# Output stage of a hybrid decoder layer: residual gate on result columns, final gain ahead of the norm, one store per row tile

## The chip, the cores and the metric

One core of one Trainium2 chip runs the whole layer as one program. The metric is the device time of one execution in microseconds; for the kernel before, three timed runs gave 243.9, 244.47 and 245.1 us (median 244.47).

## What is computed

One decoder layer for 512 tokens of width 1024, all in float32. The end of it is what the change is about:

```python
mod = c_act @ w_mod[l] + b_mod[l]
shift, scale, gate = jnp.split(mod, 3, axis=-1)
...
y_attn = rmsnorm(attn, attn_out_gain[l]) * jax.nn.silu(z_attn)
y_lru = rmsnorm(rec, lru_out_gain[l]) * jax.nn.silu(z_lru)
y = jnp.concatenate([y_attn, y_lru], axis=-1) @ w_out[l]
x = x + gate[:, None, :] * y
return rmsnorm(x, final_gain)
```

`gate` is one number per output column (1024 of them). Before this end stand the modulated norm, one input projection, block-sparse attention (8 heads) and a gated recurrence (512 channels).

## The kernel before, in words

**Tiles and stages.** Tokens are four row tiles of 128. Every large product is made exact enough by three passes: a weight or an activation `w` is split into a rounded part `wh` and a rest `wl` (function `split`: a copy that casts, then a subtraction of 1024 columns, L246, on VectorE), and `mm3` (L237 to L240) issues three matmuls. The stages are: the modulation and the norm, the first seven column blocks of the input projection (`acc`), then 17 units (`UNITS`: 13 weight blocks `wc0` to `wc12` and four of `v`) with attention (`sc` scores, `z` softmax, `tp` transposes, `av`) and the recurrence woven in, and last the output stage from `T_OUT` on.

**What sets the order.** The program is written as a list of operations with due times. `Plan.emit` (L93) is a list scheduler in the host program: it walks a clock with estimated costs, and for each engine picks the operation that can begin first and is due first. The result is one fixed order per engine and for SP's queue of transfers; the engines follow it and wait for each other by semaphores. An operation with `alt` may go to either VectorE or ScalarE. A changed cost, due time or operation anywhere can so move operations far away from it.

**The gate.** `gate_col` (L498) loads one block of the gate's weights (`wgt`, 512 KB) and multiplies it with `cb`, summing along the row (L501): 8 instructions of 128x1024 on VectorE with 8 small additions (L503). `gate_row` (L506) turns the columns into a row that stands on every partition, `grow` [128, 1024].

**The output stage** (L697 to L771). Four groups `g`: attention half times left and right columns, recurrent half times left and right columns. Each loads two blocks of `w_out` (`wo`), **multiplies them with `grow`** (L710, 8 instructions of 128x1024 on VectorE) and splits them. Then, for each row tile, 12 matmuls fill one PSUM bank `po`, and one instruction (L727) scales it by the branch's norm (`rba`, `rbl`), adds the residual `xr` and writes `xr`. In the recurrent groups ScalarE squares `xr` with a running sum (L738) into `ssq`; the left half times the final gain `fg` goes to `oa` (L743). When a row tile's right half is there, ScalarE takes the root (L750), VectorE the reciprocal (L753), ScalarE scales `oa` (L758), VectorE makes `ob` from `xr`, the norm and `fg` (L761), and each half is stored on its own (L768, L770, 256 KB each). The last row tile is cut in two at 256 columns: its second group of matmuls has 256 columns, and it leaves in four stores of 128 KB, one of them on ScalarE's queue (L765).

Of the kernel before, what the change touches and what calls it, by code (L numbers as in the profile page):

```python
# [56 lines left out]
class Plan:  # L57
# [35 lines left out]
    def emit(self, make):  # L93
# [80 lines left out]
def tile_hymba_block(ctx: ExitStack, tc: tile.TileContext, x, wss, wgt, win0, wv, winr,  # L174
# [460 lines left out]
    for n in range(3):  # L635
        recur(n, T_REST + 44.47 + n)
    for j in range(8):
        gate_col(j, T_REST + 38.31 + 6.64 * j)
# [4 lines left out]
    t_att = [T_REST + 13.0 + 5.8 * n if n < 8 else
# [55 lines left out]
    branch_rms("a", T_OUT + 2)
    for g in range(4):  # L700
        br, half = "al"[g // 2], g % 2
        s = slice(half * 512, (half + 1) * 512)
# [4 lines left out]
        for j in range(2):
            w = t4(f"wo{g}{j}", F32, (128, 2, 512))
            load(w, wo[2 * g + j], t0 - 11 + 2 * j)
            op("V", dv(1024), lambda w=w, s=s: V.tensor_mul(  # L710
                w[:], w[:], grow[:, None, s].to_broadcast([128, 2, 512])), [w, grow], [w], t0 - 7 + 2 * j)
            wos.append(split(w, like(w), f"wo{g}{j}", 1024, t0 - 5 + 2 * j))
        for t in range(NT):
            m = slice(t * 128, (t + 1) * 128)
            cuts = (0, 256, 512) if g == 3 and t == NT - 1 else (0, 512)
            for n, (lo, up) in enumerate(zip(cuts, cuts[1:])):
                ps, w = bank("po"), up - lo
                c0, c1 = half * 512 + lo, half * 512 + up
                t1 = t0 + 2.6 * t + 2.6 * lo / 512
                for k in range(4):  # L720
                    yh, yl = Y[br, k]
                    wh, wl = wos[k // 2]
                    op("PE", 3 * pe(w), lambda k=k, ps=ps, yh=yh, yl=yl, wh=wh, wl=wl, m=m, lo=lo, up=up: mm3(
                        ps[:, :up - lo], yh[:, m], yl[:, m], wh[:, k % 2, lo:up], wl[:, k % 2, lo:up], k == 0, k == 3),
                       [yh, yl, wh, wl], [ps], t1 + 0.65 * k * w / 512)
# [4 lines left out]
                if br == "a":  # L730
                    continue
                o, q = t2("o"), half + n
                if w < 512:
                    op("V", dv(w, 1), lambda t=t, c0=c0, c1=c1, o=o, q=q: V.scalar_tensor_tensor(
                        o[:, :c1 - c0], res[t][:, c0:c1], 1.0, res[t][:, c0:c1], op0=OP.mult, op1=OP.mult,
                        accum_out=ssq[t][:, q:q + 1]), [res[t]], [ssq[t], o], t1 + 0.2)
                else:
# [2 lines left out]
                if half == 0:  # L740
                    op("V", 0.1, lambda t=t: V.tensor_scalar(
                        ssq[t][:, 0:1], ssq[t][:, 0:1], 1.0 / D, EPS, op0=OP.mult, op1=OP.add), [ssq[t]], [ssq[t]], t1 + 4)
                    op("V", dv(512), lambda t=t: V.tensor_mul(outa[t][:], res[t][:, 0:512], fg[:, 0:512]),  # L743
                       [res[t], fg], [outa[t]], t1 + 5)
                elif c1 < D:
                    op("V", 0.1, lambda t=t, q=q: V.scalar_tensor_tensor(
                        ssq[t][:, 0:1], ssq[t][:, q:q + 1], 1.0 / D, ssq[t][:, 0:1], op0=OP.mult, op1=OP.add),
                       [ssq[t]], [ssq[t]], t1 + 0.6)
                else:
                    op("A", 0.2, lambda t=t, q=q: A.activation(ssq[t][:, 3:4], ssq[t][:, q:q + 1], AF.Sqrt,  # L750
                                                               bias=ssq[t][:, 0:1], scale=1.0 / D),
                       [ssq[t]], [ssq[t]], t1 + 0.3, "sqrt")
                    op("V", 0.1, lambda t=t: V.reciprocal(ssq[t][:, 3:4], ssq[t][:, 3:4]), [ssq[t]], [ssq[t]], t1 + 0.4)  # L753
                    step = 256 if t == NT - 1 else 512
                    t1 += 1.5 if t == NT - 2 else 0.0
                    for e in range(0, 512, step):
                        sa, sb = slice(e, e + step), slice(512 + e, 512 + e + step)
                        op("A", ac(step, 1), lambda t=t, sa=sa: A.activation(  # L758
                            outa[t][:, sa], outa[t][:, sa], AF.Copy, scale=ssq[t][:, 3:4]),
                           [ssq[t], outa[t]], [outa[t]], t1 + 1.5)  # L760
                        op("V", dv(step, 1), lambda t=t, sa=sa, sb=sb: V.scalar_tensor_tensor(  # L761
                            outb[t][:, sa], res[t][:, sb], ssq[t][:, 3:4], fg[:, sb], op0=OP.mult, op1=OP.mult),
                           [res[t], ssq[t], fg], [outb[t]], t1 + 1.5)
                        if t == NT - 1 and e:
                            op("A", 0.1, lambda t=t, sa=sa: A.dma_start(out[t * 128:(t + 1) * 128, sa], outa[t][:, sa]),  # L765
                               [outa[t]], [], t1 + 2)
                        else:
                            op("SP", step / 700, lambda t=t, sa=sa: SP.dma_start(  # L768
                                out[t * 128:(t + 1) * 128, sa], outa[t][:, sa]), [outa[t]], [], t1 + 2)
                        op("SP", step / 700, lambda t=t, sa=sa, sb=sb: SP.dma_start(  # L770
                            out[t * 128:(t + 1) * 128, sb], outb[t][:, sa]), [outb[t]], [], t1 + 2)  # L771
# [75 lines left out]
```

## Time and profile before

| | |
|---|---|
| Timed runs | 243.9, 244.47, 245.1 us |
| The profiled execution | 246.51 us, of which the span from first to last instruction is 244.7 us |
| TensorE busy | 228.2 us, 93% of the span |
| VectorE busy | 208.4 us, 85% |
| ScalarE busy | 159.7 us, 65% |
| Granted clock, mean | 0.994 of full speed |

All places in time below are microseconds from the start of that span. The profiled execution's 246.51 us are 2.0 us above the median of the timed runs; 1.8 us of it lie outside the span.

### The profile page before, as it was taken

To read this page: it belongs to the slowest core of one execution; us is meant where nothing else is said; L and a number is where in the kernel's file an instruction comes from. 1 tells how busy PE (TensorE), PEld (TensorE's weight loads), DVE (VectorE), ACT (ScalarE), POOL (GpSimd) and SP (SyncE) were. 2 spreads that over 40 slices of the span, in tenths; PEclk is the share of its full clock that TensorE was granted. 3 is DMA by queue.
4 is the path that set the end of the run, shared out by engine and by line. 5 is a ranking of instruction groups with operands and counts; after the bars stand their busy time and mean duration, and the time that the engine had idled before them with its cause. 6 is when DMAs were issued, how large, how long until landed. Compare 5 with 4: busy or idle time off the path is not lost.

```text
span 244.7 us, 3163 instructions
## 1 busy us (share of the span) xinstructions
PE 228.2 (93%) x1076; PEld 181.6 (74%) x1076; DVE 208.4 (85%) x419; ACT 159.7 (65%) x273; POOL 6.6 (3%) x30
## 2 busy tenths in 40 slices
PE   1679999999999999999799999999999999999990
PEld 1557888888888778678577787867776888888880
DVE  2699999957998998898999999779899999956564
ACT  5686666842748899999951488867999530312362
POOL 0000000045000000000000000000000000000000
PEclk9999999999999999999999999999999999999997
DMA  6999999910292169931528228873650000000035
GB/s 176 342 415 411 419 409 412 410 71 3 55 265 71 39 171 385 392 127 47 171 43 214 88 43 228 331 258 108 212 197 3 0 0 0 0 3 0 1 148 195
DMA packets 13551, 41.98 MB, mean 172 GB/s; under 512 B 1632, under 2 KB 2272, under 8 KB 13024
## 3 DMA queue, kind: packets, MB, share of 16 engines
q1 hardware_dynamic: 13392, 41.66, 48.7%
q8 instruction: 8, 0.13, 0.2%
q10 hardware_dynamic: 144, 0.13, 0.2%
q14 instruction: 7, 0.06, 0.1%
HBM read 35.50 MB, written 2.10 MB: 154 GB/s over the span
## 4 chain that ended last, share of the span: by engine, by line
PE 82%; ACT 9%; DVE 4%; DMA 2%; issue 1%; SPq 1%; ACTq 0%
PE acc L394 17%; PE pj L238 11%; PE pj L240 11%; PE pj L239 10%; PE po L238 6%; PE po L240 6%; PE po L239 6%; PE tp L570 3%; PE av L560 3%; DMA x<-in_x_dram 2%; PE sc L533 2%; PE sc L530 2%; PE xp L336 2%; ACT L541 2%; ACT z L541 1%; PE gt L238 1%
## 5 line engine op out<-in xcount | busy, mean ns | idle before, releaser
L541 ACT ACTIVATE z<-z,mn 128x128 f32<-128x128 f32 (+3 forms) x32 | 17.8, 560 | 1.5 <-DVE mn L538 1.4
L538 DVE CUSTOM_DVE_ANT_0 z<-sc,cst 128x128 f32<-128x128 f32 (+3 forms) x32 | 14.8, 486 | 3.3 <-PE sc L533 3.3
L363 DVE SCALAR_TENSOR_TENSOR ws<-ws,cb 128x1024 f32<-128x1024 f32 x14 | 17.1, 1228 | 0.0
L738 ACT ACTIVATE o<-xr 128x512 f32<-128x512 f32 x7 | 4.4, 633 | 11.8 <-DVE xr L727 11.8
L228 ACT COPY pt<-tp 128x128 f32<-128x128 f32 (+3 forms) x28 | 10.3, 419 | 2.7 <-PE tp L570 2.5
L541 ACT ACT_TABLE_LOAD x9 | 11.5, 1283 | 0.1
L570 PE MATMUL tp<-ident,z 128*128 128x128 f32 x80 | 11.6, 273 | 0.0
L727 DVE SCALAR_TENSOR_TENSOR xr<-po,rbl,xr 128x512 f32<-128x512 f32 (+1 forms) x9 | 6.2, 691 | 6.3 <-PE po L240 6.2
L570 PEld LDWEIGHTS tp<-ident,z 128*128 128x128 f32 x80 | 9.6, 140 | 2.5 <-issue 0.2
L501 DVE SCALAR_TENSOR_TENSOR wgt<-wgt,cb 128x1024 f32<-128x1024 f32 x8 | 9.8, 1219 | 0.0
L710 DVE TENSOR_TENSOR wo<-wo,grow 128x1024 f32<-128x1024 f32 x8 | 9.8, 1219 | 0.0
L560 PE MATMUL av<-pt,v 128*64 128x512 f32 (+3 forms) x64 | 9.6, 439 | 0.0
L462 DVE SCALAR_TENSOR_TENSOR xc<-xl,vec,xc 128x511 f32<-128x511 f32 (+2 forms) x12 | 9.0, 747 | 0.1
L590 ACT ACT_TABLE_LOAD x7 | 9.0, 1283 | 0.1
L549 DVE TENSOR_SCALAR z<-z,rs 128x384 f32<-128x384 f32 (+3 forms) x23 | 8.4, 393 | 0.6
L336 PE MATMUL xp<-ident,x 128*128 128x128 f32 x28 | 6.7, 427 | 2.0 <-DVE x L332 2.0
L560 PEld LDWEIGHTS av<-pt,v 128*64 128x64 f32 x64 | 4.8, 136 | 5.0 <-issue 3.9
L336 PEld LDWEIGHTS xp<-ident,x 128*128 128x128 f32 x28 | 5.6, 224 | 3.2 <-DVE x L332 2.8
L550 ACT ACTIVATE z<-z,rs 128x128 f32<-128x128 f32 (+3 forms) x9 | 4.8, 530 | 4.3 <-DVE rs L544 4.2
L308 PE MATMUL cp<-ident,ccol 128*128 128x128 f32 x8 | 1.9, 424 | 5.0 <-DMA ident<-in_consts_dram 5.0
L590 ACT ACTIVATE sz<-pj 128x512 f32<-128x512 f32 x8 | 4.8, 599 | 2.1 <-PE pj L240 2.0
L541 ACT ACTIVATION_READ_ACCUMULATOR z<-z,mn 128x1 f32 x32 | 6.1, 191 | 0.0
(1087 smaller groups left out, 764.7 us busy)
## 6 DMA issues: line engine op xcount, KB each, us to landing
wc<-in_winr_dram SPq DMA_DIRECT2D x13, 512.0 KB, 5.5
ws<-in_wss_dram SPq DMA_DIRECT2D x4, 1024.0 KB, 11.0
wgt<-in_wgt_dram SPq DMA_DIRECT2D x8, 512.0 KB, 6.0
wo<-in_wo_dram SPq DMA_DIRECT2D x8, 512.0 KB, 4.4
w<-in_win_dram SPq DMA_DIRECT2D x8, 448.0 KB, 9.0
ws<-in_wss_dram SPq DMA_DIRECT2D x6, 512.0 KB, 8.4
x<-in_x_dram SPq DMA_DIRECT2D x4, 512.0 KB, 6.5
wv<-in_wv_dram SPq DMA_DIRECT2D x4, 512.0 KB, 11.7
```

What stands on the lines that cost most here:

```text
L228: op("A", acp(n) if psum else ac(n), lambda: A.copy(dst(), src()), r, w, due, after=after, alt=("V", dv(n) if psum else dv2(n), lambda: V. ...
L238: PE.matmul(ps, lh, rh, start=start, stop=False)
L239: PE.matmul(ps, lh, rl, start=False, stop=False)
L240: PE.matmul(ps, ll, rh, start=False, stop=stop)
L336: op("PE", 0.2, lambda t=t, d=d: PE.transpose(xps[d][:, t * 128:(t + 1) * 128], xt[t][:, d * 128:(d + 1) * 128], ident[:]), [xt[t], ident] ...
L363: op("V", dv(1024), lambda d=d, j=j, sc=sc: V.scalar_tensor_tensor(part(d, j), part(d, j), 1.0, cb[:], op0=OP.mult, op1=OP.mult, accum_out ...
L394: PE.matmul(acc[j][:], a[:, j * 128:(j + 1) * 128], b[:], start=first, stop=last),
L538: op("V", dv(n) + 0.085, lambda s=s, z=z: V.tensor_tensor_reduce(out=z[:, :n], in0=ps[s][:, :n], in1=cst[:, 1536 - n:1536], op0=OP.add, op ...
L541: op("A", ac(n, 1, 1), lambda s=s, z=z: A.activation(z[:, :n], z[:, :n], AF.Exp, bias=mn[s][:, 0:1], scale=-1.0, accum_out=sm[:, s:s + 1]) ...
L560: PE.matmul(ps2[64 * s:64 * s + 64, k * 128:], vt[k][:, (2 * p + s) * 64:(2 * p + s + 1) * 64], pts[s][:, k, k * 128:], start=(k == 0), st ...
L570: PE.transpose(tp[:, k * 128:(k + 1) * 128], z[:, k * 128:(k + 1) * 128], ident[:])
L590: op("A", acp(512), lambda: A.activation(z[:], ps[:], AF.Silu), [ps], [z], due, "silu")
```

## The change

Five things are done:

1. `wo` is no longer multiplied with `grow`. Instead the result is: for the attention groups (`attention_part`) ScalarE or VectorE copies `po` out with the branch norm into a tile `ua` (L717, L718), VectorE multiplies it with `grow` (L719) and adds it to `xr` (L720); for the recurrent groups (`recurrent_part`) one VectorE instruction makes `u` = po x norm x `grow` (L725) and another adds it to `xr` (L729).
2. The final gain is multiplied in before the norm for both halves: `ot` = `xr` x `fg` (L732).
3. When the norm is known, one instruction of 128x1024 scales `ot` in place: on ScalarE for row tiles 0 to 2 (L753), on VectorE for the last (L750), and one store of 512 KB per row tile sends it (L756): three on SP's queue, that of row tile 2 on ScalarE's. Row tile 2 is scaled after the last row tile's root.
4. The last row tile is cut at 320 columns and not at 256; both squares are on ScalarE.
5. Due times: the 8 `gate_col` are due from `T_OUT - 52` on in steps of 6, which is `T_REST + 75.84` in the scheduler's clock (before: from `T_REST + 38.31` in steps of 6.64), `gate_row` 2 us after `T_OUT` and not 23.5 before it; the output stage's own due times are stretched a little; the attention branch's squares may no longer go to VectorE.

```diff
-        gate_col(j, T_REST + 38.31 + 6.64 * j)
-    gate_row(0, T_OUT - 23.51)
-    gate_row(1, T_OUT - 23.51 + 2)
+        gate_col(j, T_OUT - 52 + 6 * j)
+    gate_row(0, T_OUT + 2)
+    gate_row(1, T_OUT + 3)
...
+    def attention_part(t, c, ps, t1):
+        u, r = scaled[t], rb["a"]
+        op("A", acp(512, 1), lambda: A.activation(u[:, c], ps[:], AF.Copy, scale=r[:, t:t + 1]), [ps, r], [u], t1,
+           alt=("V", dv(512, 1), lambda: V.tensor_scalar(u[:, c], ps[:], r[:, t:t + 1], None, op0=OP.mult)))
+        op("V", dv(512), lambda: V.tensor_mul(u[:, c], u[:, c], grow[:, c]), [u, grow], [u], t1 + 8)
+        op("V", dv(512), lambda: V.tensor_add(res[t][:, c], res[t][:, c], u[:, c]), [u, res[t]], [res[t]], t1 + 9)
+    def recurrent_part(t, c, q, ps, t1):
+        op("V", dv(w, 1), lambda: V.scalar_tensor_tensor(
+            u[:, :w], ps[:, :w], r[:, t:t + 1], grow[:, c], op0=OP.mult, op1=OP.mult), [ps, r, grow], [u], t1)
...
+        op("V", dv(w), lambda: V.tensor_add(res[t][:, c], res[t][:, c], u[:, :w]), [u, res[t]], [x1], t1 + 0.1)
+        op("A", ac(w, 0, 1), lambda: A.activation(o[:, :w], res[t][:, c], AF.Square, accum_out=ssq[t][:, q:q + 1]),
...
+        op("V", dv(w), lambda: V.tensor_mul(ot[t][:, c], res[t][:, c], fg[:, c]), [x1, res[t], fg, *([ot[t]] if q else [])],
...
+    def send(t, t1):
+        n, i, o, last = ssq[t], Buf("view", None), Buf("view", None), t == NT - 1
+        op("V", 0.1, lambda: V.reciprocal(n[:, 3:4], n[:, 3:4]), [n, normed[t]], [i], t1 + 0.6)
+        if last:
+            op("V", dv2(D, 1), lambda: V.tensor_scalar(ot[t][:], ot[t][:], n[:, 3:4], None, op0=OP.mult),
+               [i, n, ot[t], *products[t]], [o], t1 + 1.2)
+        else:
+            op("A", ac(D, 1), lambda: A.activation(ot[t][:], ot[t][:], AF.Copy, scale=n[:, 3:4]),
+               [i, n, ot[t], *products[t]] + ([normed[NT - 1]] if t == NT - 2 else []), [o], t1 + 5.5)
+        q, queue = (A, "A") if t == NT - 2 else (SP, "SP")
+        op(queue, 0.4, lambda: q.dma_start(out[t * 128:(t + 1) * 128, :], ot[t][:]), [ot[t], o], [], t1 + (1.7 if last else 6.0))
...
-            op("V", dv(1024), lambda w=w, s=s: V.tensor_mul(
-                w[:], w[:], grow[:, None, s].to_broadcast([128, 2, 512])), [w, grow], [w], t0 - 7 + 2 * j)
...
-            cuts = (0, 256, 512) if g == 3 and t == NT - 1 else (0, 512)
+            cuts = (0, 320, 512) if g == 3 and t == NT - 1 else (0, 512)
...
-                op("V", dv(w, 1), lambda t=t, ps=ps, c0=c0, c1=c1, br=br: V.scalar_tensor_tensor(
-                    res[t][:, c0:c1], ps[:, :c1 - c0], rb[br][:, t:t + 1], res[t][:, c0:c1], op0=OP.mult, op1=OP.add),
-                   [ps, rb[br], res[t]] + ([ssq[t - 1]] if n else []), [res[t]], t1)
```

**How the order moves: VectorE in the middle of the kernel, from unit 2 of the input projection on.** `wc4` is the weight block of the fifth `wc` unit; `wc4h` is its cast, `wc4l` its rest, which the third matmul of that unit needs. Two pieces of the difference, the earlier place first:

```order
 L475 TENSOR_TENSOR gate<-gate,xc 128x512
-L229 CAST wc3h<-wc_935 128x1024
+L229 CAST wc4h<-wc_983 128x1024
 L584 SCALAR_TENSOR_TENSOR y<-av,vec,sz 128x512
 L544 RECIPROCAL rs<-sum 128x2
-L549 TENSOR_SCALAR z<-z,rs 128x128
-L229 CAST ya0h<-y 128x512
+L549 TENSOR_SCALAR z<-z,rs 128x128 x2
+L246 TENSOR_TENSOR wc4l<-wc_983,wc4h 128x1024
 L246 TENSOR_TENSOR ya0l<-y,ya0h 128x512
```

```order
 L428 STREAM_SHUFFLE sh<-pj 128x512
-L246 TENSOR_TENSOR wc4l<-wc_990,wc4h 128x1024
 L429 TENSOR_TENSOR ra<-pj,cst 128x512
 L430 TENSOR_TENSOR sh<-sh,cst 128x512
-L501 SCALAR_TENSOR_TENSOR wgt,gcol<-wgt,cb 128x1024
 L431 TENSOR_TENSOR ra<-ra,sh 128x512 x2
```

The rest of `wc4` moves up by 35 rows of the order, to before the scans and the rotation of unit 4, and its cast moves from ScalarE to VectorE; the gate's products (L501) leave this stretch, the first of the eight now standing behind the scores of head pair 2.

**SP's queue and ScalarE at the scores of head pair 2.** `k2s`, `q2s` are copies inside the chip that the scores need; `wc_1322` of the change and `wc_1360` of before are the loads that the next cast on ScalarE waits for (`wc8h` in the change, `wc9h` before). SP of before, then of the change:

```order
L447 DMA k2s<-k2hl 128x1x512
L447 DMA q2s<-q2hl 128x1x512
L235 DMA wc_1360<-in_winr_dram 128x1024
L235 DMA wc_1447<-in_winr_dram 128x1024
L447 DMA k3s<-k3hl 128x1x512
```

```order
L447 DMA k2s<-k2hl 128x1x512
L447 DMA q2s<-q2hl 128x1x512
L235 DMA wgt<-in_wgt_dram 128x1024
L235 DMA wc_1322<-in_winr_dram 128x1024
L235 DMA wgt<-in_wgt_dram 128x1024
L235 DMA wc_1383<-in_winr_dram 128x1024
```

ScalarE of the change at that place:

```order
L576 ACTIVATE sq<-av 128x512
L228 CAST wc8h<-wc_1322 128x1024
L541 ACTIVATE z,sum<-z,mn 128x128 x2
L550 ACTIVATE z<-z,rs 128x128
L228 COPY pt_1393<-tp 128x128
L228 COPY pt_1395<-tp 128x128
```

A load of `wgt` now stands between the copies and the load that ScalarE's cast waits for, and the exponentials (L541) of the first score block stand behind that cast, as they did behind `wc9h` before.

**VectorE at the very end**, of the change (`xr_1821`, `ot_2257`, `ssq_2260` belong to the last row tile):

```order
L725 SCALAR_TENSOR_TENSOR u<-po,rbl,grow 128x320
L748 RECIPROCAL ssq_2238<-ssq_2238 128x1
L729 TENSOR_TENSOR xr_1821<-xr_1821,u 128x320
L725 SCALAR_TENSOR_TENSOR u<-po,rbl,grow 128x192
L729 TENSOR_TENSOR xr_1821<-xr_1821,u 128x192
L732 TENSOR_TENSOR ot_2257<-xr_1821,fg 128x320
L736 TENSOR_SCALAR ssq_2260<-ssq_2260 128x1
L732 TENSOR_TENSOR ot_2257<-xr_1821,fg 128x192
L748 RECIPROCAL ssq_2260<-ssq_2260 128x1
L750 TENSOR_SCALAR ot_2257<-ot_2257,ssq_2260 128x1024
```

Where one instruction took `po` into `xr`, two now do; the products with the final gain stand beside the squares on ScalarE, and the last instruction scales all 1024 columns.

## Rows read from the trace of the kernel before

**Rows 1.** The page: busy time, share of the span and instructions of the engines; TensorE's busy tenths in 40 slices.

```profile
PE 228.2 (93%) x1076; PEld 181.6 (74%) x1076; DVE 208.4 (85%) x419; ACT 159.7 (65%) x273; POOL 6.6 (3%) x30
PE   1679999999999999999799999999999999999990
```

**Rows 2.** All waits of TensorE of over a few tenths: who was waited for, us in total, times, longest.

```profile
PE cp L308 <- DMA ident<-in_consts_dram: 5.0, 1, 5.0
PE xp L336 <- DVE x L332: 2.0, 2, 1.2
PE pj L240 <- DVE wc4l L246: 1.6, 1, 1.6
PE acc L394 <- ACT h0h L386: 1.6, 1, 1.6
```

**Rows 3.** Timelines around that third wait: TensorE's matmul that waited (start, duration, in brackets the idle time and its releaser), VectorE's subtraction, and ScalarE's cast of the same block.

```profile
121.79 0.50 PE L240 MATMUL pj<-h0h,wc4l 128*128 128x512 f32 x1 [1.62 <-DVE wc4l L246]
...
120.53 1.21 DVE L246 TENSOR_TENSOR wc4l<-wc,wc4h 128x1024 fp32r<-128x1024 f32 x1
...
115.86 1.03 ACT L228 CAST wc4h<-wc 128x1024 fp32r<-128x1024 f32 x1
```

**Rows 4.** Two stretches of the output stage: busy time of PE, PEld, DVE, ACT and POOL with instruction counts, granted clock, share of the DMA engines, GB/s.

```profile
195.00:217.00 22.00, 22.00 (x100) 18.21 (x99) 21.65 (x26) 5.83 (x7) 0.00 (x0) 1.00 0.00 1
217.00:236.00 19.00, 19.00 (x90) 15.89 (x91) 9.16 (x19) 6.22 (x17) 0.00 (x0) 1.00 0.08 28
```

**Rows 5.** Groups of instructions by shape: count, busy time, mean ns of one, idle time before them.

```profile
L710 DVE TENSOR_TENSOR wo<-wo,grow 128x1024 f32<-128x1024 f32 x8 | 9.8, 1219 | 0.0
L727 DVE SCALAR_TENSOR_TENSOR xr<-po,rba,xr 128x512 f32<-128x512 f32 x8 | 6.0, 748 | 0.1
L541 ACT ACTIVATE z<-z,mn 128x128 f32<-128x128 f32 x8 | 3.1, 393 | 1.0 <-DVE mn L538 1.0
L743 DVE TENSOR_TENSOR oa<-xr,fg 128x512 f32<-128x512 f32 x4 | 2.8, 692 | 0.1
L332 DVE TENSOR_SCALAR x<-x,ss 128x1024 f32<-128x1024 f32 x3 | 2.3, 754 | 0.1
L738 ACT ACTIVATE o<-xr 128x512 f32<-128x512 f32 x7 | 4.4, 633 | 11.8 <-DVE xr L727 11.8
L738 ACT ACTIVATION_READ_ACCUMULATOR o<-xr 128x1 f32 x7 | 1.3, 187 | 0.0
L758 ACT ACTIVATE oa<-oa,ssq 128x512 f32<-128x512 f32 x3 | 2.2, 724 | 1.1 <-DVE ssq L753 1.1
```

**Rows 6.** Timelines at the scores of head pair 2: SP's last copy and the loads behind it (start, time to issue; the last row holds two loads), TensorE's first scores and the transposes that need their softmax, ScalarE's cast that waited for the load; then, of the copies of `q2s`, the time from issue to landing.

```profile
128.75 0.68 SPq L447 DMA_DIRECT2D q2s<-q2hl  x1
129.52 5.62 SPq L235 DMA_DIRECT2D wc<-in_winr_dram  x2
...
133.87 0.33 PE L530 MATMUL sc<-k2s,q2s 128*128 128x128 f32 x2
134.39 0.51 PE L238 MATMUL pj<-h5h,wc5h 128*128 128x512 f32 x1
136.92 0.39 PE L533 MATMUL sc<-k2hl,q2hl 64*128 64x256 f32 x2
140.37 0.38 PE L570 MATMUL tp<-ident,z 128*128 128x128 f32 x2
...
134.75 1.05 ACT L228 CAST wc9h<-wc 128x1024 fp32r<-128x1024 f32 x1 [3.73 <-DMA wc<-in_winr_dram]
...
DMA to landing us min/median/max: 3.1/3.6/4.2
```

**Rows 7.** The end: of the chain of waits the last matmul and what follows it (start, us), then timelines of VectorE, ScalarE and SP's queue.

```profile
238.38 0.13 PE po L240
238.51 0.03 issue
...
238.54 0.48 DVE L727 SCALAR_TENSOR_TENSOR xr<-po,rbl,xr 128x256 f32<-128x256 f32 x1
239.06 0.43 DVE L734 SCALAR_TENSOR_TENSOR o<-xr 128x256 f32<-128x256 f32 x1
239.53 0.30 ACT L750 ACTIVATE ssq<-ssq 128x1 f32<-128x1 f32 x1 [0.28 <-DVE o L734]
240.07 0.16 DVE L753 RECIPROCAL ssq<-ssq 128x1 f32<-128x1 f32 x1
240.26 0.88 DVE L761 SCALAR_TENSOR_TENSOR ob<-xr,ssq,fg 128x256 f32<-128x256 f32 x2
241.22 0.93 SPq L770 DMA_DIRECT2D out_dram<-ob x2
```

**Rows 8.** Transfers: size and median us from issue to landing of the stores; of the gate's loads of 512 KB the least, median and greatest; and two stretches (columns as in rows 4), one of loads alone and one of the last stores.

```profile
out_dram<-ob SPq DMA_DIRECT2D x3, 256.0 KB, 2.0
out_dram<-ob SPq DMA_DIRECT2D x2, 128.0 KB, 2.2
...
DMA to landing us min/median/max: 3.1/6.0/8.4
...
15.00:30.00 15.00, 13.39 (x49) 10.58 (x48) 14.77 (x29) 10.47 (x15) 0.00 (x0) 1.00 1.03 415
241.00:243.50 2.50, 0.00 (x0) 0.00 (x0) 0.15 (x1) 0.17 (x1) 0.00 (x0) 0.64 0.92 315
```

More of the change, by code (lines that the diff above doesn't have):

```diff
@@ L140, in emit @@
             for b in o.w:
-                if b.tile is None:
+                if b.tile is None and b.pool != "view":
                     if b.pool in heap:
@@ L697, in tile_hymba_block, with project @@
     ssq = [fix(f"ssq{t}", [128, 4]) for t in range(NT)]
-    outa, outb = [t2(f"oa{t}") for t in range(NT)], [t2(f"ob{t}") for t in range(NT)]
+    scaled, ot = [t4(f"ua{t}") for t in range(NT)], [t4(f"ot{t}") for t in range(NT)]
+    products, squares = [[] for _ in range(NT)], [[] for _ in range(NT)]
+    ssum, normed = [Buf("view", None) for _ in range(NT)], [Buf("view", None) for _ in range(NT)]
     branch_rms("a", T_OUT + 2)
+    def project(g, t, lo, up, wos, t1):
+        br, m, w, ps = "al"[g // 2], slice(t * 128, (t + 1) * 128), up - lo, bank("po")
+        for k in range(4):
+            yh, yl = Y[br, k]
+            wh, wl = wos[k // 2]
+            op("PE", 3 * pe(w), lambda k=k, yh=yh, yl=yl, wh=wh, wl=wl: mm3(
+                ps[:, :w], yh[:, m], yl[:, m], wh[:, k % 2, lo:up], wl[:, k % 2, lo:up], k == 0, k == 3),
+               [yh, yl, wh, wl], [ps], t1 + 0.68 * k * w / 512)
+        return ps
@@ new lines, in recurrent_part @@
+    def recurrent_part(t, c, q, ps, t1):
+        w, u, o, r = c.stop - c.start, t2("u"), t2("o"), rb["l"]
+        op("V", dv(w, 1), lambda: V.scalar_tensor_tensor(
+            u[:, :w], ps[:, :w], r[:, t:t + 1], grow[:, c], op0=OP.mult, op1=OP.mult), [ps, r, grow], [u], t1)
+        x1, o1, s1 = (Buf("view", None) for _ in range(3))
+        squares[t].append(s1)
+        op("V", dv(w), lambda: V.tensor_add(res[t][:, c], res[t][:, c], u[:, :w]), [u, res[t]], [x1], t1 + 0.1)
+        op("A", ac(w, 0, 1), lambda: A.activation(o[:, :w], res[t][:, c], AF.Square, accum_out=ssq[t][:, q:q + 1]),
+           [x1, res[t]] + ([ssq[t]] if q else []), [o, s1] if q else [o, s1, ssq[t]], t1 + 0.2)
+        op("V", dv(w), lambda: V.tensor_mul(ot[t][:, c], res[t][:, c], fg[:, c]), [x1, res[t], fg, *([ot[t]] if q else [])],
+           [o1] if q else [o1, ot[t]], t1 + (0.9 if c.stop == D and t == NT - 1 else 2.6 if t == NT - 1 else 4.8))
+        products[t].append(o1)
+        if c.stop < D:
+            op("V", 0.1, lambda: V.tensor_scalar(ssq[t][:, 0:1], ssq[t][:, q:q + 1], 1.0 / D, ssq[t][:, 0:1] if q else EPS,
+                                                 op0=OP.mult, op1=OP.add),
+               [ssq[t], s1], [ssum[t]], t1 + 0.8)
@@ L700, in tile_hymba_block @@
     for g in range(4):
         br, half = "al"[g // 2], g % 2
-        s = slice(half * 512, (half + 1) * 512)
-        t0 = T_OUT + g * 10.4
+        t0 = T_OUT + g * 10.93
         if g == 2:
@@ L716, in tile_hymba_block @@
+            t1 = t0 + 2.73 * t
             for n, (lo, up) in enumerate(zip(cuts, cuts[1:])):
[L717 to L725, printed above, removed]
@@ L740, in tile_hymba_block @@
[L740 to L771, printed above, removed]
```

27 lines of the change are left out of this document (16 added, 11 removed).

## The prediction, made before the changed kernel ran

> **What bounds the kernel now.** I read the page first. TensorE is busy for 93% of the span and full in every slice from the fourth to the last but one, save the twentieth [rows 1], so time before the end can only come out of TensorE's own waits. The list of those waits has four entries [rows 2]: three belong to the start, which the change does not touch, and one of 1.6 us is in the middle, where the third matmul of a unit wants `wc4l` and VectorE is late with it. The timelines say why [rows 3]: the cast of that block was begun on ScalarE at 115.86, so that its result was there at 116.9, but VectorE began the subtraction only at 120.53, 3.6 us after that, for its order puts other work first. The two stretches of the output stage [rows 4] show TensorE full in both (22.00 of 22, 19.00 of 19), VectorE nearly full in the first (21.65 of 22) and half idle in the second (9.16 of 19). VectorE does not hold TensorE up there, full as it is. The granted clock is 1.00, the higher level of 2.4 GHz, in both.
>
> The second thing that sets the end is the tail: the last matmul is over at 238.51 [rows 7] and the span ends at 244.7, so 6.2 us lie behind TensorE's last result, in a chain from the scaled residual to the squares, the root, the reciprocal, the scaling and the stores.
>
> **The change part by part.** A change of 0.5%, 1.22 us, is about what a measurement of this kernel can tell from none.
>
> *The products `wo` x `grow` go*: 8 x 1.219 us = 9.8 us of VectorE [rows 5]. None of it is on the path, as TensorE is full beside it [rows 4]. In their place come, per row tile and half, two instructions more on the attention side (8 x 2 x 0.69 by the row of L743), one more on the recurrent side (8 x 0.69), 4 more products with `fg` less the 4 separate `ob` (about even), and part of the copies from `po` [rows 5]. That is more VectorE work in all than the 9.8 us, but it falls where VectorE has 9.8 us free in 19 [rows 4]. TensorE's matmuls are the same ones (320 and 192 columns instead of 256 and 256). Cost on the path: 0; if the cover went, TensorE would wait for PSUM banks.
>
> *The gate's columns move later.* This takes the load off VectorE that stands between unit 2 and unit 4, and in the changed order the subtraction for `wc4l` stands 35 rows earlier, with its cast beside it on VectorE. The wait of 1.62 us [rows 3] should go whole. **Term 1: -1.6 us.** Bounds: -1.6, the row of the wait itself, and 0, if another block's rest is as late in its stead.
>
> *SP's queue.* The gate's loads that left now stand around head pair 2 and 3. What is late next: ScalarE's cast of `wc8h`, with the first exponentials of head pair 2 behind it, and behind those the transposes on TensorE. In the kernel before, the same place was held by `wc9h`: its load was issued at 129.52, right behind the last copy of `q2s`, and ScalarE stood still for 3.73 us and began the cast at 134.75, 0.88 after TensorE's first scores at 133.87 [rows 6]. Now one more load of 512 KB is ahead: 0.524 MB at 415 GB/s [rows 8] is 1.26 us. Counted from the first scores: cast begins at 0.88 + 1.26 = 2.1, ends at 3.2 (1.05 us), two exponentials of 0.39 us each [rows 5] bring 4.0, reciprocal and scaling about 0.4 more: 4.4. TensorE, in the changed order, does the scores, 12 matmuls and the second scores before it wants the transposes: from 133.87 to 134.39 (0.5), 12 x 0.22 (22.00 us for 100 in rows 4: 2.6), and the second pair of scores (two of 0.39: 0.8), 3.9 in all. Before, it had 6.5 us for the same (140.37 less 133.87). That makes TensorE 0.5 late if the loads land strictly one after the other, and not late at all if the further load is half hidden under the copies before it. **Term 2: +0.2 us**, between the two; bounds 0 and +1.5 (the load one whole transfer of 1.26 later than that, on top).
>
> *The tail.* Before: 6.2 us. Now, after TensorE's last result P, with durations from rows 5 and 7, scaled by columns where the width differs: VectorE is still on the first part of the last row tile for about 0.2 (that part's matmuls end 12 x 0.10 = 1.2 us earlier, at 0.13 for 256 columns, and VectorE has 0.55 + 0.16 + 0.43 to do on it once it is through with row tile 2). Then `u` of 192 columns 0.40, the sum into `xr` 0.36 (the product row L743 is 0.69 for 512 plus its handover), square 0.37 and its read-out 0.19, root 0.30, reciprocal 0.16, scaling of 1024 columns 0.75 (L332): 2.5. Handovers: in the chain before, four steps of 0.48, 0.43, 0.30 and 0.16 = 1.37 us took from 238.54 to 240.26, so 0.35 on top. Together P + 3.1; in the kernel before, the last stores went from 241.22 on, P + 2.7. ScalarE's scaling of row tile 2 begins after the root and takes about twice L758's 0.72 less one start-up, so its store goes about 0.1 after.
>
> Then 1 MB leaves at once, where before the last two stores were 128 KB pieces. No row shows a store of 512 KB. From below: a store of 256 KB lands after 2.0, the other 0.79 MB at the loads' 415 GB/s take 1.9: 3.9. From above: at the 315 GB/s of the last stores 2.5: 4.5; and by the loads of 512 KB, 3.1 at the least plus 1.26 for the second: 4.4 [rows 8]. I take 4.0, because rows of 4 KB are what the loads move and the small pieces of 512 bytes to 2 KB are not. The span ended 0.8 after the last landing (issued at 241.7, 2.2 to landing, 244.7). Sum: 3.1 + 0.1 + 4.0 + 0.8 = 8.0, against 6.2. **Term 3: +1.8 us**, bounds +1.4 (2.8 to the issue, 3.9) and +2.5.
>
> Of the Trainium skill, "DMA: Bandwidth & Descriptors", section Specifications, gives a limit of about 358 GB/s between HBM and one core; by it the 0.79 MB would take 2.2 us, an estimate, and term 3 would be +2.1. The 415 GB/s over 15 us in rows 8 is above that, so the row decides.
>
> *The sum*: -1.6 + 0.2 + 1.8 = **+0.4 us**. Made against the profiled execution (246.51 us, span 244.7) it gives 246.9 and a span of 245.1; that execution is 2.0 above the median of the runs shown, so against the median it is 244.47 + 0.4 = **244.9 us**. What TensorE gains in the middle is lost in the stores.
>
> **The rivals.**
>
> *A. ScalarE holds TensorE (slower).* The mechanism of term 2 at full price: SP's queue puts `wgt` ahead of `wc8`, the cast waits, exponentials and transposes wait behind it in order. For it: the 3.73 us wait of the same kind [rows 6], and TensorE's room there shrinks from 6.5 to 4.0. Against: with 1.26 us more the lateness is only 0.4. It decides when the load lands more than about 1.2 us later than reckoned, which a second `wgt` or slower copies would do; then TensorE waits 1.5 here and term 3 stands: -1.6 + 1.5 + 1.8 = +1.7, 246.2 us.
>
> *B. The change doesn't free `wc4l` (slower).* If another block's rest is late in its stead, since the whole order after unit 2 is new, the 1.6 us come back: +0.2 + 1.8 = +2.0, 246.5 us. Against: the gate's products, 1.2 us each [rows 5], have left VectorE's order in that stretch.
>
> *C. The last two stores go side by side (faster).* They are on two queues. If each moved at its own rate, both would land like one of 512 KB: 2.0 + 0.26 MB / 415 GB/s = 2.6, term 3 becomes 3.2 + 2.6 + 0.8 - 6.2 = +0.4, and the sum -1.0; with a chain at its lower bound (2.8) -1.3: 243.2 us. Against: in the stretch of loads the share of the 16 DMA engines is 1.03 at 415 GB/s [rows 8], they have no second such rate to give. The Trainium skill says the same in "DMA: Bandwidth & Descriptors", section Issuing engines are not separate DMA queues: transfers of all issuers run on the same 16 engines; no run here shows two large stores on two queues.
>
> **How the numbers follow.** Forecast 0.62: its own range is 243.9 to 245.7 (terms 1 and 2 at +0.2 and 0, term 3 at its ends, and the 0.6 us by which runs scatter). A 0.17, B 0.08, C 0.13. Faster by over 0.5% is C: 0.13. Slower by over 0.5% is A and B: 0.25. Within 0.5%: 0.62. For 8 in 10 the range takes in C's price and all of A: 243.2 to 246.5.
>
> **What would show it.** Right: no wait for `wc4l` in TensorE's list; the last matmul's end near 237.1; two stores issued within 0.3 us of each other about 3 us behind it; DMA engines full for 2.5 us at about 400 GB/s; 0.2 us or so of wait at the transposes of head pair 2, ScalarE standing still before `wc8h`. Wrong: TensorE's last result later than 238 (term 1 or 2), or landing under 3.3 us after issue (term 3, rival C), or a wait of TensorE for PSUM in the output stage, which would mean that VectorE's added work was not covered.

## The result and the profile after

Four runs of the changed kernel gave 247.29 to 248.7 us, median 247.91, against 244.78 for four runs of before: ratio 1.012, interval 1.008 to 1.016. The forecast was 244.9 with a range to 246.5, so the measurement lies outside it. A second comparison, 12 runs against 35, gave 246.13 against 244.97: **ratio 1.0059, interval 1.0029 to 1.0088, or 1.4 us slower**. Both say slower. What the forecast had wrong, and how far the traces explain the gap between the two measurements, is what follows. Two single executions in the comparisons below took 265 us at a granted clock of 0.85, and the ratios leave such slow ones out.

The page after, and all waits of TensorE in it (who was waited for, us in total, times, longest):

```profile
PE 226.8 (92%) x1076; PEld 181.0 (74%) x1076; DVE 211.4 (86%) x429; ACT 164.9 (67%) x280; POOL 7.1 (3%) x30
```

```profile
PE cp L308 <- DMA ident<-in_consts_dram: 5.1, 1, 5.1
PE xp L336 <- DVE x L332: 2.2, 2, 1.4
PE acc L394 <- ACT h0h L386: 2.1, 1, 2.1
PE tp L570 <- DVE gcol L503: 1.5, 1, 1.5
```

Against [rows 2]: the wait for `wc4l` is gone as forecast, and one of the same size stands at the transposes of head pair 2. The name `gcol` must not be taken at its word. The chain that ended last shows, in order of time, what really came before it (start, us, what):

```profile
126.76 6.48 DMA wc<-in_winr_dram
...
133.26 1.05 ACT wc8h L228
134.31 0.79 ACT z L541 x4
...
135.12 0.18 DVE rs L544
...
135.32 0.29 DVE z L549
135.61 0.08 DVE gcol L503
...
135.76 0.41 PE tp L570 x2
```

The load for `wc8` lands at 133.24, the cast on ScalarE follows, behind it the exponentials, and 2.5 us after the cast's start the transposes. `gcol` is only the small VectorE instruction that happened to stand last. TensorE had been through with the second pair of scores at 134.3 (timelines of TensorE, ScalarE and SP's queue; in brackets the idle time and its releaser):

```profile
130.18 0.33 PE L530 MATMUL sc<-k2s,q2s 128*128 128x128 f32 x2
133.91 0.38 PE L533 MATMUL sc<-k2hl,q2hl 64*128 64x256 f32 x2
135.76 0.41 PE L570 MATMUL tp<-ident,z 128*128 128x128 f32 x2 [1.46 <-DVE gcol L503]
...
133.26 1.05 ACT L228 CAST wc8h<-wc 128x1024 fp32r<-128x1024 f32 x1 [5.27 <-DMA wc<-in_winr_dram]
...
124.78 0.69 SPq L447 DMA_DIRECT2D q2s<-q2hl  x1
125.51 1.15 SPq L235 DMA_DIRECT2D wgt<-in_wgt_dram  x1
126.76 1.07 SPq L235 DMA_DIRECT2D wc<-in_winr_dram  x1
127.94 0.41 SPq L235 DMA_DIRECT2D wgt<-in_wgt_dram  x1
```

The output stage in the stretches of [rows 4], with the same columns:

```profile
195.00:217.00 22.00, 22.00 (x107) 18.41 (x108) 19.35 (x27) 8.26 (x13) 0.00 (x0) 1.00 0.08 25
217.00:236.00 19.00, 19.00 (x90) 15.98 (x89) 16.45 (x28) 5.98 (x15) 0.00 (x0) 1.00 0.03 13
```

The end, which answers to [rows 7]: timelines of TensorE's last matmul, then VectorE, ScalarE and the two queues.

```profile
237.36 0.28 PE L240 MATMUL po<-wo31h,yl3l 128*128 128x192 f32 x1
238.02 0.41 DVE L725 SCALAR_TENSOR_TENSOR u<-po,rbl,grow 128x192 f32<-128x192 f32 x1
238.46 0.36 DVE L729 TENSOR_TENSOR xr<-xr,u 128x192 f32<-128x192 f32 x1
238.85 0.36 ACT L730 ACTIVATE o<-xr 128x192 f32<-128x192 f32 x1
239.77 0.16 DVE L748 RECIPROCAL ssq<-ssq 128x1 f32<-128x1 f32 x1 [0.16 <-ACT ssq L742]
239.97 0.75 DVE L750 TENSOR_SCALAR ot<-ot,ssq 128x1024 f32<-128x1024 f32 x1
238.29 2.79 SPq L756 DMA_DIRECT2D out_dram<-ot  x2
240.81 0.38 ACTq L756 DMA_DIRECT2D out_dram<-ot  x1
```

Of the four stores of 512 KB, the time from issue to landing:

```profile
DMA to landing us min/median/max: 2.6/3.0/3.9
```

TensorE stays full in the output stage while VectorE's work there rises from 9.16 to 16.45 us in the second stretch: the added VectorE work is covered. The last result stands at 237.64, SP's last store (the second of its row) leaves 0.1 before ScalarE's at 240.81, the later of the two lands 3.9 after its issue, and the span ends at 245.50: a tail of 7.9 us, where it was 6.2. The longer chain behind TensorE's last result doesn't delay the last issue: it comes 3.2 us after that result in both kernels (before: second issue of the last row of [rows 7], at 241.72). What has grown is the landing of that last store, from 2.1 to 3.9 us (SP's queue, before):

```profile
241.72 0.43 SPq L770 DMA_DIRECT2D out_dram<-ob  x1
```

### The profile page after: what moved, and what is told of

The parts are those of the page before. It is cut to its first block, busy times and chain, and to the rows that moved or that the text cites. A ratio compares the mean times of both kernels' runs of the same rounds, so it can differ in the third digit from the quotient of the medians.

```text
span 245.5 us, 3157 instructions
## 1 busy us (share of the span) xinstructions
PE 226.8 (92%) x1076; PEld 181.0 (74%) x1076; DVE 211.4 (86%) x429; ACT 164.9 (67%) x280; POOL 7.1 (3%) x30
## 4 chain that ended last, share of the span: by engine, by line
PE 87%; DMA 5%; ACT 3%; DVE 2%; SPq 0%; issue 0%; ACTq 0%
PE acc L394 16%; PE pj L238 13%; PE pj L240 12%; PE pj L239 12%; PE po L238 6%; PE po L240 6%; PE po L239 6%; PE tp L570 4%; PE av L560 4%; DMA wc<-in_winr_dram 3%; DMA x<-in_x_dram 3%; PE sc L533 2%; PE sc L530 2%; PE xp L336 2%; PE gt L238 1%; PE gt L240 1%
## 5 line engine op out<-in xcount | busy, mean ns | idle before, releaser
L541 ACT ACTIVATE z<-z,mn 128x128 f32<-128x128 f32 (+3 forms) x32 | 17.8, 556 | 2.1 <-DVE mn L538 2.0
L730 ACT ACTIVATE o<-xr 128x512 f32<-128x512 f32 (+2 forms) x9 | 5.2, 581 | 12.9 <-DVE xr L729 12.8
L228 ACT COPY pt<-tp 128x256 f32<-128x256 f32 (+3 forms) x24 | 8.7, 407 | 4.5 <-PE tp L570 4.3
L560 PE MATMUL av<-pt,v 128*64 128x512 f32 (+3 forms) x64 | 10.0, 439 | 0.0
L501 DVE SCALAR_TENSOR_TENSOR wgt<-wgt,cb 128x1024 f32<-128x1024 f32 x8 | 9.8, 1219 | 0.0
L560 PEld LDWEIGHTS av<-pt,v 128*64 128x64 f32 x64 | 5.4, 136 | 5.1 <-issue 3.4
L549 DVE TENSOR_SCALAR z<-z,rs 128x256 f32<-128x256 f32 (+3 forms) x23 | 8.4, 390 | 0.6
L717 ACT ACTIVATE ua<-po,rba 128x512 f32<-128x512 f32 x5 | 3.4, 690 | 7.5 <-PE po L240 7.5
L336 PE MATMUL xp<-ident,x 128*128 128x128 f32 x28 | 6.0, 390 | 2.2 <-DVE x L332 2.2
L725 DVE SCALAR_TENSOR_TENSOR u<-po,rbl,grow 128x512 f32<-128x512 f32 (+2 forms) x9 | 6.2, 688 | 1.5 <-PE po L240 1.5
L336 PEld LDWEIGHTS xp<-ident,x 128*128 128x128 f32 x28 | 4.9, 203 | 3.4 <-DVE x L332 3.0
L541 ACT ACTIVATION_READ_ACCUMULATOR z<-z,mn 128x1 f32 x32 | 6.0, 187 | 0.0
L729 DVE TENSOR_TENSOR xr<-xr,u 128x512 f32<-128x512 f32 (+2 forms) x9 | 5.7, 633 | 0.2
```

The costliest lines, as they stand in the source:

```text
L336: op("PE", 0.2, lambda t=t, d=d: PE.transpose(xps[d][:, t * 128:(t + 1) * 128], xt[t][:, d * 128:(d + 1) * 128], ident[:]), [xt[t], ident] ...
L501: op("V", dv(1024), lambda: V.scalar_tensor_tensor(w[:], w[:], 1.0, cb[:], op0=OP.mult, op1=OP.mult, accum_out=gcol[:, j:j + 1]), [w, cb], ...
L541: op("A", ac(n, 1, 1), lambda s=s, z=z: A.activation(z[:, :n], z[:, :n], AF.Exp, bias=mn[s][:, 0:1], scale=-1.0, accum_out=sm[:, s:s + 1]) ...
L560: PE.matmul(ps2[64 * s:64 * s + 64, k * 128:], vt[k][:, (2 * p + s) * 64:(2 * p + s + 1) * 64], pts[s][:, k, k * 128:], start=(k == 0), st ...
```

## The experiments

**How they are read.** Executions of one and the same kernel scatter by up to 4 us (242.73 to 246.77 in the twelve of `same_before`), so 1 us is hard to see in single times. The traces allow more: three stretches of the span, set by TensorE, are compared. *Start* is up to the first matmul of the last first-stage block (`acc<-h7h,w07h`, L394), *middle* from there to TensorE's last result, *tail* from that to the span's end. Worked out so from the eleven profiles, in us:

```
kernel           start   middle   tail   wait in the middle
before           54.03   184.47   6.24   1.6 wc4l
same_before      52.10   184.43   6.23   1.6 wc4l
changed          52.91   184.73   7.87   1.5 transposes
after_again      51.81   184.42   7.88   1.5 transposes
e_wc8_first      53.00   182.73   7.88   none
e_gate_early     51.52   184.57   7.87   1.6 wc4l
e_less_behind    51.79   183.93   7.88   1.0 transposes
e_old_tail       52.94   184.15   7.04   1.3 transposes
e_t2_free        51.63   184.39   7.35   1.0 transposes
e_one_queue      53.16   184.81   7.88   1.4 transposes
e_mix            53.00   182.53   6.23   none
```

Every kernel has the same program for the start, and most of the scatter lies there: 51.5 to 54.0. From the first matmul of the first block (`acc<-h0h,w00h`) on, the start takes 35.3 to 35.6 us in ten profiles and 36.7 in the first of before; the rest of the scatter lies ahead of that matmul, which begins at 16.2 to 17.6, and there TensorE's waits for `x` (L336) are 1.0 to 2.2 us in all. What makes these differ is not shown. Middle and tail repeat within 0.3 us and 0.01 us for the same program (rows 1 and 2, rows 3 and 4 of the table). Between different programs the middle less its wait still differs, from 182.5 to 183.4: in `e_t2_free` the `av` matmuls at 154 to 157 us (L560) take 0.46 longer than in `after_again`, with no wait in the list. So differences of the middle under half a microsecond are not read.

**The kernel before against itself** (no edit).

> The kernel before against itself, to see what its start costs from execution to execution. Of the 3.1 us by which the change was slower in the runs, the two traces explain about 1.9: -1.6 (no wait for wc4l) +1.5 (the wait of TensorE at the transposes of head pair 2) +0.4 (small pieces) +1.6 (the tail). Theory start: the rest is scatter of the first 25 us, where TensorE runs some microseconds at 1.2 GHz after its wait for h0h (5.5 us long in the profiled execution of before, 3.5 us in that of the change); then the ratio is 1.000 within 0.004, and the spans of the single executions scatter by 1 to 2 us while the time from 30 us to the last matmul stays at 209.0 within 0.3. Rival: the executions of before agree within 0.5 us from the start to 30 us, and the missing microsecond lies later, in the changed kernel.

Measured: 244.75 against 244.97 us, ratio 0.9992 (0.9965 to 1.0020); its middle 184.43, its tail 6.23, its start 1.9 us shorter than in the first profile. The theory "start" holds for the place: the 246.51 us of the first profiled execution were 2 us high for its start alone. It holds for 1.1 of the 1.9 us as to the cause: in that execution the matmuls of the first block follow each other at 0.43 us for 512 columns, which is 1.2 GHz, from the end of TensorE's wait of 1.6 us for `h0h`, at 17.3, to 23.0; in `same_before` only from 17.8 to 21.2, and then at 0.23, near 2.4 GHz. The other 0.8 us lie ahead of the first block, which begins at 17.32 and at 16.53. The single times scatter by 4 us and not by the 1 to 2 expected (timelines of TensorE, before and then `same_before`):

```profile
22.61 0.63 PE L394 MATMUL acc<-h0l,w00h 128*128 128x512 f32 x1
23.36 0.39 PE L394 MATMUL acc<-h0l,w00h 128*128 128x512 f32 x1
23.59 0.39 PE L394 MATMUL acc<-h0h,w00l 128*128 128x512 f32 x1
```

```profile
20.82 0.56 PE L394 MATMUL acc<-h0l,w00h 128*128 128x512 f32 x1
21.21 0.39 PE L394 MATMUL acc<-h0h,w00l 128*128 128x512 f32 x1
21.45 0.40 PE L394 MATMUL acc<-h0l,w00h 128*128 128x512 f32 x1
```

**The changed kernel once more** (no edit).

> The changed kernel once more. Theory path: +1.9 us, ratio 1.008 (1.005 to 1.011). Rival start: the changed kernel also loses at its start more often than before does, ratio 1.011 to 1.016, and its spans are longer by as much within the first 30 us.

Measured: 246.13 us, ratio 1.0059 (1.0029 to 1.0088), +1.4 us; middle 0.0 and tail +1.65 against `same_before`. The theory "path" holds, at 1.6 rather than 1.9, as the "+0.4 of small pieces" was not there again. What made the first four runs 1.8 us slower than these twelve is not shown. One of the four, 247.29 us, has a trace: against that of `after_again`, 245.89 us, its start is 1.1 longer, its middle 0.3, and the tail is the same.

**One load of `wgt` behind that for `wc8`.** The list scheduler's order is kept, and one operation is issued one place later on SP's queue:

```diff
+            if o.skip:
+                held.append(o)
+            else:
                 o.fn()
+                for b in [b for b in held if b.eng == o.eng]:
+                    b.skip -= 1
+                    if not b.skip:
+                        held.remove(b)
+                        b.fn()
...
         load(w, wgt[j], due - 6)
+        plan.ops[-1].skip = int(j == 2)
```

> The changed kernel with one load of wgt put behind the load for wc8 on SP's queue, nothing else moved. Theory queue (rival A of the prediction): the 1.46 us wait of TensorE at the transposes of head pair 2 comes from that load standing ahead; the wc8 load lands about 131.1 and not 133.2, ScalarE begins its cast 2 us earlier, the wait is under 0.2 us, and the kernel is 1.4 us faster than the changed one (ratio to before 1.002 to 1.004 if the changed one stands at 1.008). Rival: the wait comes from VectorE's product for the gate (L501), which stands ahead of the reciprocal: then the wait stays above 1 us. Second rival: the wait goes and another block's rest is late in its stead, gain under 0.5 us.

Measured: 244.62 us, ratio 0.9987 (0.9954 to 1.0020), 1.5 us under `after_again`. Middle 182.73. Timelines of ScalarE, TensorE and VectorE; the kernel's lines are shifted by 8 or 9:

```profile
131.25 1.05 ACT L236 CAST wc8h<-wc 128x1024 fp32r<-128x1024 f32 x1 [3.19 <-DMA wc<-in_winr_dram]
...
133.97 0.38 PE L542 MATMUL sc<-k2hl,q2hl 64*128 64x256 f32 x2
134.29 0.44 PE L579 MATMUL tp<-ident,z 128*128 128x128 f32 x2
...
131.29 1.22 DVE L510 SCALAR_TENSOR_TENSOR wgt<-wgt,cb 128x1024 f32<-128x1024 f32 x1
133.11 0.17 DVE L553 RECIPROCAL rs<-sum 128x2 f32<-128x2 f32 x1 [0.58 <-ACT z L550]
```

The cast begins 2 us earlier, measured from the same copies, and the transposes follow the scores without a gap. The theory "queue" is shown; VectorE's gate product (here L510) stands where it stood, ahead of the reciprocal, so the first rival falls, and no other block took over the wait: TensorE's list has none in the middle.

**The gate's columns due as before.**

```diff
-        gate_col(j, T_OUT - 52 + 6 * j)
+        gate_col(j, T_REST + 38.31 + 6.64 * j)
```

> The changed kernel with the gate's columns due when they were before; gate on the result, scaling and stores as changed. It asks whether the move of the columns is what took the wait for wc4l away and put the wait at the transposes of head pair 2 in its place. Theory move: the wait for wc4l is back at 1.5 us or so, the wait at the transposes of head pair 2 is gone, and from the first matmul of the last first-stage block to TensorE's last result it takes 184.4 to 184.8 us, as in both kernels; tail 7.9. Rival: the products that left the weights are what freed VectorE; then the wait for wc4l stays under 0.5 us and that stretch takes 183.

Measured in one execution: the wait for `wc4l` is back at 1.6, that at the transposes is gone, middle 184.57, tail 7.87. The theory "move" holds. So it is the columns' place, not the products that left the weights, which made and unmade both waits (of TensorE's waits in the middle, the only one):

```profile
PE pj L240 <- DVE wc4l L246: 1.6, 1, 1.6
```

**Fewer loads behind `wc8`.** The same mechanism as above with `skip = 2 * int(j == 3)`.

> The changed kernel with the second wgt load behind the one for wc8 put two places later, so that only one load stands behind wc8's when it moves; the first wgt load stays ahead of it. In the five profiles with the changed order the wc8 load landed 3.7 to 4.3 us after the last copy of q2s, where the prediction reckoned 1.3 more than the 1.74 of before, 3.0. Theory shared: loads issued behind it take part of the rate; with one fewer it lands 3.0 to 3.5 us after the copy and TensorE's wait is 0.2 to 0.8 us. Rival: two loads of 512 KB behind those copies take that long whatever stands behind; then 3.7 to 4.3 us again and a wait of 1.0 to 1.5 us.

Measured in one execution, on another chip than the other experiments: 3.7 us from the copy's landing to that of `wc8`, wait 1.0. By the numbers set beforehand the theory "shared" fails and the rival holds, each just so. This is no clean decision: 3.7 is better than the 4.2 of `after_again`, but `e_t2_free`, with both loads behind, had 3.75 and 1.0 as well.

**The tail of before on the changed kernel.** `ot` is scaled in halves and, for the last row tile, quarters:

```diff
-            op("V", dv2(D, 1), lambda: V.tensor_scalar(ot[t][:], ot[t][:], n[:, 3:4], None, op0=OP.mult),
...
+        for e in range(0, 512, step):
+            op("A", ac(step, 1), lambda sa=sa: A.activation(ot[t][:, sa], ot[t][:, sa], AF.Copy, scale=n[:, 3:4]),
...
+            op("V", dv(step, 1), lambda sb=sb: V.scalar_tensor_tensor(
+                ot[t][:, sb], res[t][:, sb], n[:, 3:4], fg[:, sb], op0=OP.mult, op1=OP.mult),
...
-                        if t == NT - 1:
-                            send(t - 1, t1 - 2.7)
-                        if t != NT - 2:
-                            send(t, t1)
+                        send(t, t1)
```

> The changed kernel with the last scaling and the stores as before: left half on ScalarE, right half on VectorE with the final gain in the same instruction, halves of 256 KB and for the last row tile pieces of 128 KB, row tile 2 not held back. The rest (gate on the result, its columns late) as changed. Theory stores: the tail after TensorE's last result falls from 7.9 to 6.2 or 6.4 us, 1.5 to 1.7 us faster than the changed kernel, ratio to before 1.001 to 1.002 at 1.008 for the changed one. Rival chain: the two additional VectorE instructions behind the last matmul are most of the 1.6, and the tail stays above 7 us.

Measured: ratio 1.0027 (0.9990 to 1.0064), an interval that takes in both 1 and the changed kernel's 1.0059; tail 7.04. Neither theory: the tail is above the 7 of the rival, but the chain is not "most of the 1.6". Half of the 1.64 us goes with the stores of before (7.88 to 7.04), half stays with the chain (7.04 to 6.24). The chain's half is read from VectorE, ScalarE and SP's last store (TensorE's last result is at 237.09):

```profile
237.47 0.41 DVE L725 SCALAR_TENSOR_TENSOR u<-po,rbl,grow 128x192 f32<-128x192 f32 x1
237.91 0.36 DVE L729 TENSOR_TENSOR xr<-xr,u 128x192 f32<-128x192 f32 x1
238.05 0.71 ACT L755 ACTIVATE ot<-ot,ssq 128x512 f32<-128x512 f32 x1
238.66 0.35 ACT L730 ACTIVATE o<-xr 128x192 f32<-128x192 f32 x1
239.48 0.16 DVE L749 RECIPROCAL ssq<-ssq 128x1 f32<-128x1 f32 x1 [0.42 <-ACT ssq L743]
...
241.10 0.43 SPq L762 DMA_DIRECT2D out_dram<-ot  x1
```

The reciprocal comes 2.4 after TensorE's last result, 1.6 in [rows 7]: VectorE does two instructions where one stood, and the squares wait for ScalarE to scale row tile 2. The last store leaves 4.0 after that result, where it leaves after 3.2 in before and in the changed kernel. So these halves are not the changed kernel's own: there the reciprocal comes 2.1 after the result, and one scaling and one store for the last row tile, instead of four of each, make up the time until the last issue.

**Row tile 2 not held back.**

```diff
-               [i, n, ot[t], *products[t]] + ([normed[NT - 1]] if t == NT - 2 else []), [o], t1 + 5.5)
+               [i, n, ot[t], *products[t]], [o], t1 + (1.5 if t == NT - 2 else 5.5))
```

> The changed kernel with row tile 2 scaled as soon as its own norm is known and not after the last row tile's root, so that its 512 KB leave about 1.8 us before those of row tile 3; ScalarE's scaling of 1.1 us now stands ahead of the last squares and makes the last chain some 0.4 us longer. Theory bytes: the two stores of 512 KB share the DMA engines, so a store that is alone lands in 2.6 us and not 3.3 to 3.9; the tail falls from 7.9 to 7.0 (0.4 up, 1.3 down). Rival: the stores don't disturb each other; then the tail grows to 8.2.

Measured in one execution: tail 7.35, above the 7.0 expected and below the rival's 8.2. The last store, nearly alone, as the one before it landed 0.7 after its issue, took 2.6 us, 1.3 less than the later of the pair, as the theory "bytes" says; the chain grew by 0.8, twice what was expected, since ScalarE did both scalings in a row ahead of the last squares (its timeline):

```profile
235.52 2.17 ACT L753 ACTIVATE ot<-ot,ssq 128x1024 f32<-128x1024 f32 x2
237.60 0.45 ACT L730 ACTIVATE o<-xr 128x320 f32<-128x320 f32 x1
```

Of its four stores, from issue to landing:

```profile
DMA to landing us min/median/max: 2.6/2.7/2.9
```

**Both last stores on SP's queue.**

```diff
-        q, queue = (A, "A") if t == NT - 2 else (SP, "SP")
+        q, queue = SP, "SP"
```

> The changed kernel with row tile 2's store on SP's queue too, behind that of row tile 3 (so the two last stores stand in one queue). Theory bytes: the two queues share the same 16 DMA engines, one queue lands the second store no later: 3.9 us from issue or less (3.3 for the first plus 1.3 at 400 GB/s, less what the second issue lags, 0.4), tail 7.8 to 8.1. Rival: two queues move side by side and one queue does not; then the second store lands 4.6 us or more after its issue and the tail is 8.5 or more.

Measured in one execution: tail 7.88, as with two queues. From the first issue to the last landing the two stores take 3.9 us in both, and while they move, the DMA engines are full and have the same rate in both (columns as in [rows 4]; the changed kernel, then this one):

```profile
241.50:243.90 2.40, 0.00 (x0) 0.00 (x0) 0.00 (x0) 0.00 (x0) 0.00 (x0) 0.50 0.99 394
```

```profile
241.83:244.23 2.40, 0.00 (x0) 0.00 (x0) 0.00 (x0) 0.00 (x0) 0.00 (x0) 0.50 0.99 394
```

A second queue gives no second rate. The Trainium skill, "DMA: Bandwidth & Descriptors", section Issuing engines are not separate DMA queues, says that transfers of all issuers share the 16 engines; this pair agrees.

**A version that keeps what helped.** The changed kernel with `wgt` behind `wc8`, the gate on the result in the attention groups, but on the weights in the two recurrent groups, and the tail of before:

```diff
             load(w, wo[2 * g + j], t0 - 11 + 2 * j)
+            if br == "l":
+                s = slice(half * 512, (half + 1) * 512)
+                op("V", dv(1024), lambda w=w, s=s: V.tensor_mul(
+                    w[:], w[:], grow[:, None, s].to_broadcast([128, 2, 512])), [w, grow], [w], t0 - 7 + 2 * j)
```

> A version that the two places point to: the gate's columns late and the wgt load behind wc8's, the gate on the result in the two attention groups (there it is not yet known when the weights are split), but on the weights of the two recurrent groups, with the squares, the scaling, the cuts and the stores of before. If the terms add: -1.6 in the middle against before, 0 in the tail, so 1.7 us less than before (ratio 0.993, interval 0.990 to 0.996), stretch to TensorE's last result 182.8, tail 6.2. Rival: the four products of 1.2 us on VectorE for the recurrent weights make a block of these late; then TensorE waits in the output stage and the ratio is 0.996 or more.

Measured: 243.39 against 245.37 us, ratio 0.9891 (0.9856 to 0.9926). Middle 182.53, 1.9 less than before, tail 6.23, together 1.9 us or a ratio of 0.992, inside the measured interval; the ratio itself lies a little under the 0.990 to 0.996 expected. TensorE has no wait left outside the start (all its waits), so the rival falls:

```profile
PE cp L316 <- DMA ident<-in_consts_dram: 5.2, 1, 5.2
PE xp L344 <- DVE x L340: 1.9, 2, 1.1
PE acc L402 <- ACT h0h L394: 1.9, 1, 1.9
```

In the stretches the terms add within 0.3 us (182.5 against 182.8).

## Why the prediction was wrong

- **What bounds the kernel**: right. TensorE and the tail set the time in every version. VectorE's added work in the output stage made TensorE wait nowhere; behind TensorE's last result it is on the path, as the prediction's tail has it.
- **Term 1, -1.6**: right. The wait for `wc4l` left with the columns' move, and came back with it in `e_gate_early`.
- **Term 2, +0.2: the step that failed.** TensorE's wait at the transposes of head pair 2 measured +1.5, the term's upper bound and the mechanism of rival A, which I gave 0.17. TensorE's room (3.9 reckoned, 4.1 measured) and the way from cast to transposes (2.3 and 2.5) were right. The load was mis-sized: I added 1.26 us, 512 KB at the 415 GB/s of the start, to the 1.74 that `wc9` took behind the last copy, which makes 3.0. `wgt` landed 2.1 and `wc8` 4.3 us behind that copy. The lateness reckoned, 0.5, grows by these 1.3 and falls by 0.3, as the first scores began 0.3 later behind that copy than in before: 1.5. The 415 GB/s came from loads that stream with nothing but loads beside them; here copies inside the chip went ahead and two more loads were in flight, and why the loads took longer there stays open. Then I halved the lateness by "half hidden under the copies", for which no row spoke. That was a wish, and it moved the sum by 0.3.
- **Term 3, +1.8**: right, 1.64. To the last issue 3.2 reckoned and 3.2 measured, landing 4.0 and 3.9, end 0.8 and 0.83. Before, the same three were 3.2, 2.1 and 0.95, so what was added is the landing, as the sum has it. Its upper bound, +2.5, does not come out of its rows: 3.2 + 4.5 + 0.8 - 6.2 is +2.3; and with 2.2 us for the 0.79 MB the term is +2.0, not +2.1.
- **The sum** with term 2 at its price is -1.6 + 1.5 + 1.6 = +1.5 us; against 244.47 that is 246.0, what twelve runs give (246.13) and inside the range, which reaches to 246.5. Rival A's 246.2 was the right forecast. That the first measurement lies 1.4 above the range's end is not explained by term 2. The prediction allowed 0.6 us for the scatter of runs, from three of them, where executions of one kernel scatter by 4; but all four first runs lie above all twelve later ones, the only one with a trace has 1.1 of its 1.4 us in the start, and the others have none. So the cause of this part stays open. The forecast's own range, 243.9 to 245.7, was also too narrow by its own terms: -1.6 + 0 + 1.4 - 0.6 begins at 243.7, and -1.6 + 0.2 + 2.5 + 0.6 ends at 246.2.
- **Rival B** did not happen: no other block's rest became late. **Rival C** did not happen: on two queues the stores landed after 3.3 and 3.9 us, not after 2.6 each, and one queue is no slower (`e_one_queue`).

## What to carry over

When a load moves ahead of another in a full queue, price it by the landings of loads in that very stretch, not by the best rate of the kernel, and give the mechanism the chance that its upper bound deserves when all that hides it is a fraction of a microsecond. A wait that is removed frees its time only if the next late thing has room, so look first at what the move puts in front of the next wait: here one place in the queue cost the 1.5 us again. Three runs that lie within 1.2 us of each other don't bound the scatter, which was 4 us in twelve. Large stores at the end need fewer instructions, but their bytes leave late and together.

## What the runs showed of the hardware

- After TensorE's waits at the start (5.0 to 5.5 us for `ident`, 1.0 to 2.2 for `x`, 1.6 to 2.2 for `h0h`) its matmuls of 512 columns lie 0.43 us apart, 1.2 GHz, for 2.7 to 3.8 us in ten traces and 5.7 in the first of before, and 0.23 apart behind that. The slow stretch begins with the first block or up to 1.6 us into it. The wait of 1.5 us in the middle of the changed kernel had no such effect: the matmuls behind it follow at 0.23 us, and the granted clock from 135.7 to 142 is 1.00. The granted clock shows the slow stretch in ten traces (0.50 in that of `same_before`) but not in that of before, where it reads 1.00 over matmuls 0.43 apart; that trace has no entry of it ahead of 23.2 us, so there the spacing of the matmuls is the safer sign (before, then `same_before`; columns as in [rows 4]):

```profile
17.30:23.10 5.80, 5.78 (x14) 4.58 (x15) 5.80 (x12) 4.55 (x7) 0.00 (x0) 1.00 1.02 408
```

```profile
17.80:21.10 3.30, 3.30 (x9) 2.59 (x8) 3.30 (x9) 2.16 (x4) 0.00 (x0) 0.50 1.03 409
```

- The first load of 512 KB behind the copies of `q2s` landed 1.7 to 1.8 us after the last copy in the three kernels where no other load followed within 5 us (before, `same_before`, `e_gate_early`), and 2.1 to 2.8 us after it in the eight where more loads did. The second load landed 1.4 to 2.2 us after the first with `wgt` ahead, 1.3 and 1.8 with `wc8` ahead (`e_wc8_first`, `e_mix`); at the rate of the loads in [rows 8] 512 KB take 1.26. Why, the traces don't say.
